# Lane work ordered behind each k-step's weight split, and lanes cut into more steps, in a hybrid encoder layer

## The chip, the cores and the metric

The kernel runs on one core of one Trainium2 chip. The metric is device time in microseconds (us) of that core; the time before is the median of three runs. The engines are named as the profile does: PE (TensorE, matrix multiplications and transposes; PEld its weight loads), DVE (VectorE), ACT (ScalarE), POOL (GpSimd) and SP (SyncE, which here only issues DMAs). Each engine runs its own list of instructions in the order in which the list stands; engines wait for each other and for DMAs by semaphores.

## The reference

One layer of an encoder over two groups of tokens, a sample of 1024 and a prompt of 256, with shared weights, and 256 memory tokens for each. The width is 2048. Cut to what matters:

```python
hn = rms_norm(x, norm_g)
xbc, z_ssd, dt_raw, q, k, v, z_att, mq, z_mem = split_cols(hn @ w_in, IN_SIZES)
xbc = silu(centred_dwconv(xbc, conv_w, conv_b))           # 5 taps along the tokens
y = ssd_scan(forward) + ssd_scan(backward) + d_skip * xs   # 16 heads, chunks of 128 tokens
o_ssd = rms_norm(y * silu(z_ssd), ssd_norm_g)              # in two groups
q, k = rms_norm(q), rms_norm(k)
o_att = window_attention(q, k, v, sink) * silu(z_att)      # |t-s| <= 128, ALiBi, 8 heads on 2
mk, mv = split_cols(rms_norm(mem) @ w_mem_kv)
mq, mk = rms_norm(mq), rms_norm(mk)
o_mem = softmax(mq @ mk.T / sqrt(128)) @ mv * silu(z_mem)  # 4 heads
return x + concat([o_ssd, o_att, o_mem]) @ w_out
```

## The kernel before, in words

The ten tiles of 128 tokens (eight of the sample, two of the prompt) are worked on in two groups of five. The large products (input projection, memory projection, output projection) are a stream of *blocks* on PE. A block takes 16 k-steps of 128 input features. Both operands are split into a high and a low part of type float32r, and each product is three matmuls: high by high, high by low, low by high. The activations of a group lie split in SBUF in four quarters (`xH`, `xL`). The weights come in k-step by k-step: SP loads `wraw` (four buffers), `wsplit` makes `wh` of it on ACT (a copy to float32r, L219, or L222 with a gain) and `wl` on DVE (the rest, L220 or L223); both have three buffers, so the split of a k-step waits until PE is done with the k-step three before it. `block_tok` (tokens on the output's partitions, up to five accumulators, matmuls L269 to L271) and `block_feat` (features on the partitions, two k-steps at a time, matmuls L304 to L306) put the matmuls out. The last two k-steps of a block are done accumulator by accumulator, and each accumulator is evicted by a function of the block's own (`ev_gate`, `ev_gateT`, `ev_raw`, `ev_dtkv`, `ev_conv`, `ev_out`, `ev_mk`, `ev_mv`), mostly to DRAM, through tiles with the tags `evt` and `evu`, two buffers each. PSUM has five buffers for accumulators (`acc`) and three for all else (`mix`).

Blocks follow each other in this order: `mk` and `mv` for the memory, then for the first group q, kv, za (2 blocks), x (6 blocks), mq, zm (2), z0, z1; for the second group kv, x (6), z0, z1, q, za (2), mq, zm (2); then four blocks of the output projection for each group.

Everything between those products is *lane work*, written as Python generators and put into two queues (`lanes`): `mem_stats` and `x_stats` (sums of squares of the rows), `vectors` and `distances` (constants), `mk_prep` and `k_prep` (norm, split and transposition of keys), `dt_prep`, `attn` (window attention of a tile of tokens), `mem_attn`, `ssd_up` (the forward scan, the diagonal part and the states of a chunk) and `ssd_down` (the backward scan and the gate). A `yield` ends a lane's *step*. `run` draws the matmuls of a block, and after each k-step `pump` lets the lanes go on, in turns, by as many steps as the rate of the block allows (`RATES`, steps for each k-step; halved in `block_feat`, which yields twice for each pair). `need` runs a lane's steps at once where its result must be there. So a program order is recorded: the split of a k-step, its matmuls, lane steps, the next split.

The order on each engine is not the recorded order. A scheduler places the instructions of each engine by priority and by its own estimate of when operands are ready. `tc.high_priority(offset=100)` moves the priority of the splits forward by 100 instructions. Nothing ties lane instructions to a split: a lane instruction whose operands are ready early in that estimate may stand on its engine long before the splits that were recorded ahead of it. Its load, DMA-issued by SP, stands on SP in the same manner.

In the lanes that the change touches, these lines matter: `mk_prep` loads a tile (L424), squares it on ACT (L428), sums it on DVE (L429), takes the inverse root on POOL (`rsqrt`, L133 and L134) and scales on DVE (L432, L433), all in one step, then leaves four steps before the transposition on PE. `k_prep` (ACT L466, DVE L467, L471, L472), `attn` (ACT L571, DVE L573, L577) and `mem_attn` (ACT L672, DVE L674, L678, PE L684) begin in the same way. `ssd_up` loads `bc` and `xc` three steps before PE uses them (L775), and its inner function `weights` loads two rows of decays, `rf` and `rb`, to all partitions, leaves one step, then adds a bias to each of 2 x 4 quarters on ACT (L848), merges them on DVE (L849) and takes the Exp on ACT (L850); `diag` multiplies with the result (L858). `vectors` loads eight constants and has `aneg` go through an Exp on ACT four steps later (L1024). `fill_transposed` (L193, L196) and `fill_direct` (L210 to L214), which fill the quarters of the next activations, are not lane steps; `run` calls them between k-steps.

Of the kernel before, what the change touches and what calls it, by code (L numbers as in the profile page):

```python
# [10 lines left out]
F32 = mybir.dt.float32  # L11
# [5 lines left out]
ALU = mybir.AluOpType  # L17
# [10 lines left out]
SCR = 1024  # L28
CH, WB, RB, WA, WBB = 3, 3, 4, 5, 4
RBB = 3  # L30
RATES = ({'kv': 1.7, 'q': 1.5, 'za': 1.5, 'x': 1.5, 'mq': 2.52, 'zm': 1.8, 'z0': 2.17, 'z1': 1.26},
         {'kv': 0.84, 'x': 1.35, 'z0': 3.81, 'z1': 2.6, 'q': 2.65, 'za': 0.93, 'mq': 2.9, 'zm': 2.54,
          'o': 2.6})
NEG = -1e30

C_X, C_Z, C_DT, C_Q, C_K, C_V, C_ZA, C_MQ, C_ZM = 0, 1536, 2560, 2592, 3104, 3232, 3360, 3872, 4384
# [4 lines left out]
def hymba_encoder_kernel(  # L41
# [106 lines left out]
    def queue(lane, fn, ts):  # L148
        for t in ts:
            lanes[lane].append(((fn.__name__, t), fn(t)))  # L150

    def step(lane):
        name, gen = lane[0]
        try:
            next(gen)
        except StopIteration:
            lane.popleft()
            done.add(name)
# [57 lines left out]
    def wsplit(raw, h, l, g=None):  # L216

        if g is None:
            A.activation(h, raw, AF.Copy)  # L219
            V.tensor_sub(l, raw, h.bitcast(F32))  # L220
        else:
            A.activation(h, raw, AF.Copy, scale=g)  # L222
            V.scalar_tensor_tensor(out=l, in0=raw, scalar=g, in1=h.bitcast(F32), op0=ALU.mult, op1=ALU.subtract)  # L223

    def w_laid(src, n, gain=None):

# [109 lines left out]

    def ev_raw(dst, base):
        def f(i, ps):
            z = ev.tile([P, 512], F32, tag="evu", name="qs")
            A.activation(z, ps, AF.Copy)  # L340
            S.dma_start(dst[base + i], z)
        return f

    def ev_dtkv(base):
        def f(i, ps):
            t = base + i
            rt = rx[:, t:t + 1]
            r = ev.tile([P, P], F32, tag="evu", name="kraw")
            A.activation(r, ps[:, 32:160], AF.Copy, scale=rt)
            S.dma_start(k_d[t], r)  # L350
            V.scalar_tensor_tensor(out=dt_all[:, t, :], in0=ps[:, :32], scalar=rt, in1=dtb, op0=ALU.mult, op1=ALU.add)
            V.tensor_scalar(out=v_all[:, i + (2 if base else 0), :], in0=ps[:, 160:288], scalar1=rt, scalar2=None,
                            op0=ALU.mult)
        return f
# [52 lines left out]
        return mp.tile([P, 512], F32, tag="wa", name=name, bufs=WA)  # L407

    def ev_mk(i, ps):
        kr = ev.tile([P, 512], F32, tag="evu", name="mkr")  # L410
        A.activation(kr, ps, AF.Copy)
        S.dma_start(mq_d[i], kr)

# [8 lines left out]
    def mk_prep(i):  # L422
        kr = w2("mkr")
        S.dma_start(kr, mq_d[i])  # L424
        ss = sm.tile([P, 4], F32, tag="s4", name="ss", bufs=4)
        sq = w2("sq")
        rm = rx[:, 10 + i:11 + i]
        A.activation(sq, kr, AF.Square, scale=rm)  # L428
        V.reduce_sum(out=ss, in_=hv(sq, 4), axis=AX.X)  # L429
        r = sm.tile([P, 4], F32, tag="s4", name="r", bufs=4)  # L430
        rsqrt(r, ss, 1.0 / P, 4)
        V.scalar_tensor_tensor(out=hv(kr, 4), in0=hv(kr, 4), scalar=rm, in1=hb(r, 4, P), op0=ALU.mult, op1=ALU.mult)  # L432
        V.tensor_mul(hv(kr, 4), hv(kr, 4), gm.unsqueeze(1).broadcast_to([P, 4, P]))  # L433
        for _ in range(4):
            yield
        ps = psum("pmk")
        for h in range(4):
            T.transpose(ps[:, h * P:(h + 1) * P], kr[:, h * P:(h + 1) * P], ident)
        c = slice((i % 2) * P, (i % 2) * P + P)
        if i < 2:  # L440
            A.activation(mkH[:, :, c], hv(ps, 4), AF.Copy)
            V.tensor_sub(mkL[:, :, c], hv(ps, 4), mkH[:, :, c].bitcast(F32))
        else:
            o = w2("mko")
            A.activation(o, ps, AF.Copy)
            S.dma_start(mk_d[:, :, c], hv(o, 4))
        yield
# [13 lines left out]
    def k_prep(t):  # L461
        r = w2("kr")[:, :P]
        S.dma_start(r, k_d[t])
        ss = sm.tile([P, 2], F32, tag="s2", name="kss", bufs=4)
        sq = w2("ksq")[:, :P]
        A.activation(sq, r, AF.Square)  # L466
        V.reduce_sum(out=ss, in_=hv(sq, 2), axis=AX.X)  # L467
        rr = sm.tile([P, 2], F32, tag="s2", name="krr", bufs=4)
        rsqrt(rr, ss, 1.0 / 64, 2)
        r3 = hv(r, 2)  # L470
        V.tensor_mul(r3, r3, hb(rr, 2, 64))  # L471
        V.tensor_mul(r3, r3, gq.unsqueeze(1).broadcast_to([P, 2, 64]))  # L472

        kh = mp.tile([P, 4, 2, 64], F32R, tag="wa", name="kh", bufs=WA)
        for d in range(2):
            A.activation(kh[:, 0:2, d, :], r3, AF.Copy)
        for d in range(2):
            V.tensor_sub(kh[:, 2:4, d, :], r3, kh[:, 0:2, 0, :].bitcast(F32))
        yield
        yield  # L480
        ps = psum("pk")
        kf = kh.rearrange("p a b d -> p (a b d)")
        for a in range(4):
            T.transpose(ps[:, a * P:(a + 1) * P].bitcast(F32R), kf[:, a * P:(a + 1) * P], identr)
        sl = t if t < 5 else t - 3
        c = slice(sl * P, (sl + 1) * P)
        V.tensor_copy(kT[:, :, c], hv(ps[:, :256], 2))
        A.activation(kL[:, :, c], hv(ps[:, 256:], 2), AF.Copy)
        yield
# [69 lines left out]
    def attn(t):  # L559
# [7 lines left out]
        tc_ = slice(ti * P, (ti + 1) * P)  # L567
        q = w2("q")
        S.dma_start(q, q_d[t])
        sq = w2("sq")  # L570
        A.activation(sq, q, AF.Square, scale=rx[:, t:t + 1])  # L571
        ss = sm.tile([P, 8], F32, tag="s8", name="qss", bufs=4)
        V.reduce_sum(out=ss, in_=hv(sq), axis=AX.X)  # L573
        r = sm.tile([P, 8], F32, tag="s8", name="qr", bufs=4)
        rsqrt(r, ss, 1.0 / 64, 8)
        q3 = hv(q)
        V.scalar_tensor_tensor(out=q3, in0=q3, scalar=rx[:, t:t + 1], in1=hb(r, 8, 64), op0=ALU.mult, op1=ALU.mult)  # L577
        yield
        yield
        yield  # L580
        qT = []
        for b in range(2):
# [83 lines left out]
    def mem_attn(t):  # L666
        grp, ti = divmod(t, 5)
        tc_ = slice(ti * P, (ti + 1) * P)
        q = w2("mq")
        S.dma_start(q, mq_d[t])  # L670
        sq = w2("sq")
        A.activation(sq, q, AF.Square, scale=rx[:, t:t + 1])  # L672
        ss = sm.tile([P, 4], F32, tag="s4", name="mss", bufs=4)
        V.reduce_sum(out=ss, in_=hv(sq, 4), axis=AX.X)  # L674
        r = sm.tile([P, 4], F32, tag="s4", name="mr", bufs=4)
        rsqrt(r, ss, 1.0 / P, 4)
        q3 = hv(q, 4)
        V.scalar_tensor_tensor(out=q3, in0=q3, scalar=rx[:, t:t + 1], in1=hb(r, 4, P), op0=ALU.mult, op1=ALU.mult)  # L678
        yield
        yield  # L680
        yield
        ps = psum("pmq")
        for h in range(4):
# [74 lines left out]
    def ssd_up(t):  # L758
# [6 lines left out]
        for g in range(2):  # L765
            x = wb("xc", shape=(P, 4, P))
            S.dma_start(x, xbc_d[4 * g:4 * g + 4, :, tok].rearrange("f p c -> p f c"))
            xc.append(x)
        yield
        yield  # L770
        yield

        ps = psum("pcb")
        for g in range(2):
# [26 lines left out]
        for g in range(2):  # L801
# [22 lines left out]
            if not first:  # L824
# [4 lines left out]
                S.dma_start(sb_d[t][:, c], st)  # L829
                yield  # L830
        mts = {}

        def weights(q):
            g = q // 2

            rf = mp.tile([P, 512], F32, tag="rf", name="rf", bufs=2)
            mt = mp.tile([P, 512], F32, tag="rb", name="rb", bufs=RBB)
            r0 = 32 * (t % 5) + 4 * q
            for d, r in enumerate((rf, mt)):
                S.dma_start(r, ac_d[t // 5][r0 + 16 * d:r0 + 16 * d + 4, :]  # L840
                            .rearrange("h c -> (h c)").partition_broadcast(P))
            yield

            for d, r in enumerate((rf, mt)):
                for j in range(4):
                    c = slice(j * P, (j + 1) * P)
                    h = 16 * d + 4 * q + j
                    A.activation(r[:, c], r[:, c], AF.Identity, bias=wj_all[:, t, h:h + 1])  # L848
            V.copy_predicated(hv(mt, 4), upper.bitcast(U32).unsqueeze(1).broadcast_to([P, 4, P]), hv(rf, 4))  # L849
            A.activation(mt, mt, AF.Exp)  # L850
            V.tensor_mul(hv(mt, 4), hv(mt, 4), cb[:, g, :].unsqueeze(1).broadcast_to([P, 4, P]))
            mts[q] = mt

        def diag(g):
# [9 lines left out]
            V.tensor_add(ya[g], ya[g], py)  # L864
            S.dma_start(yp_d[t][:, g * 512:(g + 1) * 512], ya[g])

        for q in range(3):
            yield from weights(q)
            yield
        diag(0)  # L870
        yield
        yield from weights(3)
        yield
        yield
        diag(1)
# [136 lines left out]
    def vectors(_):  # L1012
        gk, gmk = w2("gk")[:, :64], w2("gmk")[:, :P]
        for t, a in ((gq, q_norm_g[0]), (gk, k_norm_g[0]), (gm, mq_norm_g[0]), (gmk, mk_norm_g[0]),
                     (dskip, d_skip[0]), (sinkb, sink[0]), (dtb, dt_bias.rearrange("o a h -> (o a h)")),
                     (aneg, a_log.rearrange("o a h -> (o a h)"))):
            S.dma_start(t, a.partition_broadcast(P))
        yield
        yield
        yield  # L1020
        yield
        V.scalar_tensor_tensor(out=gq, in0=gq, scalar=64 ** -0.5, in1=gk, op0=ALU.mult, op1=ALU.mult)
        V.scalar_tensor_tensor(out=gm, in0=gm, scalar=P ** -0.5, in1=gmk, op0=ALU.mult, op1=ALU.mult)
        A.activation(aneg, aneg, AF.Exp)  # L1024
        V.tensor_scalar(out=aneg, in0=aneg, scalar1=-1.0, scalar2=None, op0=ALU.mult)
        yield
# [153 lines left out]
```

## Time and profile before

| what | us |
|---|---|
| median of three runs | 1917.64 (1916.83 to 1919.4) |
| profiled execution, its own time | 1925.01 |
| profiled execution, span of the core | 1923.3 |
| PE busy | 1875.9 (98% of the span) |
| DVE busy | 1049.4 (55%) |
| ACT busy | 760.9 (40%) |
| POOL busy | 81.6 (4%) |
| DMA, mean share of 16 engines on the main queue | 48.9% |

The span runs from the first to the last instruction. Busy time is a union, so overlapping matmuls count once. The views used below are the page of the profile, the view of waits (who waited for whom, total, times and longest), the order of time of one engine in a stretch, and the table of stretches with the busy time and count of each engine, the clock granted to PE (1.00 is full), the share of the DMA engines and GB/s.

### The profile page before, as it was taken

The page shows a single profiled execution, that of the slowest core. Times are in us where ns is not written, and L with a number is a line of the kernel's source. Part 1 is how long each engine was busy: PE and PEld are TensorE (multiplying, and loading weights), DVE is VectorE, ACT ScalarE, POOL GpSimd, SP SyncE. Part 2 cuts the span into 40 slices and gives each one's busy share as a digit, 9 for nine tenths or more (in the row PEclk, how much of TensorE's full clock was granted, in tenths as well). Part 3 has the DMA queues.
Part 4 walks back from the last instruction along what each step waited for, and adds up shares of the span by engine and source line. Part 5 has one row for each costly group of instructions (what it writes and reads, how often), then busy time and mean ns, then how long its engine had stood idle before and what let it go on. Part 6 is the DMA issues. An engine that isn't in the chain of part 4 may idle for free.

```text
span 1923.3 us, 28675 instructions
## 1 busy us (share of the span) xinstructions
PE 1875.9 (98%) x10568; PEld 1634.2 (85%) x10568; DVE 1049.4 (55%) x2133; ACT 760.9 (40%) x1721; POOL 81.6 (4%) x147
## 2 busy tenths in 40 slices
PE   8999989999999999999999999999999999999999
PEld 6779989998898879999978778978978787778887
DVE  4443646677564555667776554576675454542222
ACT  6462463333452545423436444334453333421121
POOL 1010010000000000000100000000000000000000
PEclk9999999999999999999999999999999999999999
DMA  8683563233343545433444567655555345454432
GB/s 272 198 257 104 157 182 121 85 114 109 116 124 113 154 140 172 138 96 101 140 131 142 158 177 247 209 187 162 170 158 186 123 149 159 136 176 132 133 120 69
DMA packets 191340, 289.40 MB, mean 150 GB/s; under 512 B 18977, under 2 KB 68193, under 8 KB 191201
## 3 DMA queue, kind: packets, MB, share of 16 engines
q1 hardware_dynamic: 191056, 287.53, 48.9%
q8 instruction: 83, 1.36, 0.3%
q14 instruction: 57, 0.46, 0.1%
q10 hardware_dynamic: 144, 0.06, 0.0%
HBM read 230.59 MB, written 56.92 MB: 149 GB/s over the span
## 4 chain that ended last, share of the span: by engine, by line
PE 77%; DMA 11%; ACT 4%; DVE 4%; issue 2%; POOL 1%; SPq 1%; ACTq 0%; DVEq 0%; POOLq 0%
PE acc L269 14%; PE acc L270 14%; PE acc L271 14%; PE acc L304 8%; PE acc L305 8%; PE acc L306 8%; DMA xst<-in_x_sample_dram 2%; DMA rf<-ac 2%; PE po L648 2%; PE py L858 1%; PE ppt L637 1%; DMA rb<-ac 1%; DVE wl L220 1%; PE pst L826 1%; PE pst L817 1%
## 5 line engine op out<-in xcount | busy, mean ns | idle before, releaser
L269 PE MATMUL acc<-wh,xH 128*128 128x512 f32 (+1 forms) x1568 | 619.0, 395 | 9.0 <-ACT wh L219 5.6
L270 PE MATMUL acc<-wl,xH 128*128 128x512 f32 (+1 forms) x1568 | 601.6, 384 | 2.9 <-DVE wl L220 2.7
L271 PE MATMUL acc<-wh,xL 128*128 128x512 f32 (+1 forms) x1568 | 600.3, 383 | 0.0
L220 DVE TENSOR_TENSOR wl<-wraw,wh 128x512 fp32r<-128x512 f32 (+1 forms) x416 | 278.3, 670 | 384.4 <-ACT wh L219 376.1
L219 ACT ACTIVATE wh<-wraw 128x512 fp32r<-128x512 f32 (+1 forms) x416 | 254.1, 612 | 528.7 <-PE acc L271 268.0
L304 PE MATMUL acc<-xH,wh 128*128 128x320 f32 x1280 | 406.1, 317 | 9.0 <-DVE zs L331 4.7
L306 PE MATMUL acc<-xH,wl 128*128 128x320 f32 x1280 | 396.6, 310 | 1.6 <-DVE wl L220 1.4
L305 PE MATMUL acc<-xL,wh 128*128 128x320 f32 x1280 | 396.6, 310 | 0.0
L269 PEld LDWEIGHTS acc<-wh,xH 128*128 128x128 f32 x1568 | 296.4, 189 | 69.2 <-issue 8.4
L270 PEld LDWEIGHTS acc<-wl,xH 128*128 128x128 f32 x1568 | 296.7, 189 | 62.9 <-issue 6.6
L271 PEld LDWEIGHTS acc<-wh,xL 128*128 128x128 f32 x1568 | 296.2, 189 | 56.5 <-issue 0.6
L304 PEld LDWEIGHTS acc<-xH,wh 128*128 128x128 f32 x1280 | 241.3, 189 | 15.0 <-DVE zs L331 5.2
L305 PEld LDWEIGHTS acc<-xL,wh 128*128 128x128 f32 x1280 | 241.3, 189 | 3.3 <-issue 3.2
L306 PEld LDWEIGHTS acc<-xH,wl 128*128 128x128 f32 x1280 | 241.1, 188 | 2.3 <-DVE wl L220 2.3
L223 DVE SCALAR_TENSOR_TENSOR wl<-wraw,vec,wh 128x512 fp32r<-128x512 f32 x64 | 48.0, 750 | 128.0 <-ACT wh L222 128.0
L222 ACT ACTIVATE wh<-wraw,vec 128x512 fp32r<-128x512 f32 x64 | 46.3, 723 | 145.4 <-PE acc L271 132.3
L379 DVE SCALAR_TENSOR_TENSOR c<-u,vec,c 128x638 f32<-128x638 f32 (+1 forms) x96 | 84.5, 880 | 1.0
L848 ACT ACTIVATE rb<-rb,wj_all 128x128 f32<-128x128 f32 x160 | 53.0, 391 | 49.1 <-DMA rb<-ac 46.5
L848 ACT ACTIVATE rf<-rf,wj_all 128x128 f32<-128x128 f32 x160 | 53.6, 390 | 33.5 <-DMA rf<-ac 33.5
L622 ACT ACTIVATE lg<-lg,nm 128x384 f32<-128x384 f32 (+1 forms) x80 | 45.1, 564 | 46.2 <-DVE nm L616 46.1
L849 DVE COPY_PREDICATED rb<-upper,rf 128x512 f32<-128x512 uint32 x40 | 30.3, 757 | 53.0 <-ACT rb L848 52.8
L214 DVE SCALAR_TENSOR_TENSOR xL<-chd,vec,xH 128x640 fp32r<-128x640 f32 (+1 forms) x48 | 39.6, 837 | 23.5 <-ACT xH L213 23.5
(238 smaller groups left out, 1725.5 us busy)
## 6 DMA issues: line engine op xcount, KB each, us to landing
wraw<-in_w_in_laid_dram SPq DMA_DIRECT2D x288, 256.0 KB, 2.8
wraw<-in_w_out_laid_dram SPq DMA_DIRECT2D x128, 256.0 KB, 2.7
chd<-in_x_turned_dram SPq DMA_DIRECT2D x32, 320.0 KB, 4.1
rf<-ac SPq DMA_DIRECT2D x40, 256.0 KB, 3.8
rb<-ac SPq DMA_DIRECT2D x40, 256.0 KB, 4.2
out_dram<-yt SPq DMA_DIRECT2D x40, 256.0 KB, 3.6
wraw<-in_w_mem_laid_dram SPq DMA_DIRECT2D x32, 256.0 KB, 4.3
xst<-in_x_sample_dram SPq DMA_DIRECT2D x32, 256.0 KB, 4.9
```

Source lines behind the costliest of these rows:

```text
L219: A.activation(h, raw, AF.Copy)
L220: V.tensor_sub(l, raw, h.bitcast(F32))
L222: A.activation(h, raw, AF.Copy, scale=g)
L223: V.scalar_tensor_tensor(out=l, in0=raw, scalar=g, in1=h.bitcast(F32), op0=ALU.mult, op1=ALU.subtract)
L269: T.matmul(ps[t][:, :n], sh, h[:, :n], start=(k_ == 0), stop=False)
L270: T.matmul(ps[t][:, :n], sh, l[:, :n], start=False, stop=False)
L271: T.matmul(ps[t][:, :n], sl, h[:, :n], start=False, stop=(k_ == KT - 1))
L304: T.matmul(o, sh, cur["H", q][:, m, c], start=(k == 0), stop=False)
L305: T.matmul(o, sh, cur["L", q][:, m, c], start=False, stop=False)
L306: T.matmul(o, sl, cur["H", q][:, m, c], start=False, stop=(k == KT - 1))
L379: V.scalar_tensor_tensor(out=c[:, :n], in0=u[:, k:k + n], scalar=cw[k], in1=c[:, :n], op0=ALU.mult, op1=ALU.add)
L848: A.activation(r[:, c], r[:, c], AF.Identity, bias=wj_all[:, t, h:h + 1])
```

## The change

Four things are changed. `wsplit` keeps its two instructions in `marks`, and each lane step is recorded inside `tc.issue_after` for both: every ACT instruction of the step gets an ordering edge behind that k-step's `wh`, and every DVE instruction one behind its `wl`. No semaphore comes with the edge; it only sets the order on the engine. Second, lanes get further `yield`s between a load, POOL's inverse root and their users, `ssd_up` splits `weights` into `rows` (the loads, one call ahead) and `weights` (the rest), waits six steps instead of three for `bc` in tiles 0 and 4, and `vectors` waits six. Third, `ev_raw`, `ev_dtkv` and `ev_mk` alternate between the tags `evt` and `evu`. Fourth, the rates are set anew, most of them higher.

```diff
-RATES = ({'kv': 1.7, 'q': 1.5, 'za': 1.5, 'x': 1.5, 'mq': 2.52, 'zm': 1.8, 'z0': 2.17, 'z1': 1.26},
-         {'kv': 0.84, 'x': 1.35, 'z0': 3.81, 'z1': 2.6, 'q': 2.65, 'za': 0.93, 'mq': 2.9, 'zm': 2.54,
-          'o': 2.6})
+RATES = ({'kv': 1.8, 'q': 1.7, 'za': 1.7, 'x': 1.7, 'mq': 2.7, 'zm': 1.9, 'z0': 2.4, 'z1': 1.6},
+         {'kv': 1.0, 'x': 1.4, 'z0': 3.7, 'z1': 2.8, 'q': 2.8, 'za': 1.3, 'mq': 2.8, 'zm': 2.4,
+          'o': 2.65})
...
+    marks = []
+
     def step(lane):
         name, gen = lane[0]
         try:
-            next(gen)
+
+            with ExitStack() as st:
+                for ins in marks:
+                    st.enter_context(tc.issue_after(ins))
+                next(gen)
         except StopIteration:
...
     def wsplit(raw, h, l, g=None):
 
         if g is None:
-            A.activation(h, raw, AF.Copy)
-            V.tensor_sub(l, raw, h.bitcast(F32))
+            a = A.activation(h, raw, AF.Copy)
+            b = V.tensor_sub(l, raw, h.bitcast(F32))
...
+        marks[:] = a.ins, b.ins
...
     def ev_raw(dst, base):
         def f(i, ps):
-            z = ev.tile([P, 512], F32, tag="evu", name="qs")
+            z = ev.tile([P, 512], F32, tag="evt" if i % 2 else "evu", name="qs")
...
     def mk_prep(i):
         kr = w2("mkr")
         S.dma_start(kr, mq_d[i])
+        yield
...
         rsqrt(r, ss, 1.0 / P, 4)
+        yield
+        yield
         V.scalar_tensor_tensor(out=hv(kr, 4), in0=hv(kr, 4), scalar=rm, in1=hb(r, 4, P), op0=ALU.mult, op1=ALU.mult)
         V.tensor_mul(hv(kr, 4), hv(kr, 4), gm.unsqueeze(1).broadcast_to([P, 4, P]))
-        for _ in range(4):
-            yield
+        yield
+        yield
...
     def k_prep(t):
         S.dma_start(r, k_d[t])
+        yield
...
         rsqrt(rr, ss, 1.0 / 64, 2)
+        yield
...
     def attn(t):   # and mem_attn(t) in the same way
         S.dma_start(q, q_d[t])
+        yield
...
         rsqrt(r, ss, 1.0 / 64, 8)
+        yield
         q3 = hv(q)
         V.scalar_tensor_tensor(out=q3, in0=q3, scalar=rx[:, t:t + 1], in1=hb(r, 8, 64), op0=ALU.mult, op1=ALU.mult)
-        yield
-        yield
         yield
...
     def ssd_up(t):
-        yield
-        yield
-        yield
+        for _ in range(6 if t in (0, 4) else 3):
+            yield
...
-        for q in range(3):
-            yield from weights(q)
-            yield
-        diag(0)
-        yield
-        yield from weights(3)
-        yield
-        yield
-        diag(1)
-        yield
+        rows(0)
+        yield
+        for q in range(3):
+            if q < 2:
+                rows(q + 1)
+                yield
+            weights(q)
+            yield
+        diag(0)
+        rows(3)
+        yield
+        yield
+        weights(3)
+        yield
+        yield
+        diag(1)
+        yield
...
     def vectors(_):
-        yield
-        yield
-        yield
-        yield
+        for _ in range(6):
+            yield
         V.scalar_tensor_tensor(out=gq, in0=gq, scalar=64 ** -0.5, in1=gk, op0=ALU.mult, op1=ALU.mult)
         V.scalar_tensor_tensor(out=gm, in0=gm, scalar=P ** -0.5, in1=gmk, op0=ALU.mult, op1=ALU.mult)
+        yield
         A.activation(aneg, aneg, AF.Exp)
```

More of the change, by code (lines that the diff above doesn't have):

```diff
@@ L218, in wsplit @@
         if g is None:
-            A.activation(h, raw, AF.Copy)
-            V.tensor_sub(l, raw, h.bitcast(F32))
-        else:
-            A.activation(h, raw, AF.Copy, scale=g)
-            V.scalar_tensor_tensor(out=l, in0=raw, scalar=g, in1=h.bitcast(F32), op0=ALU.mult, op1=ALU.subtract)
+            a = A.activation(h, raw, AF.Copy)
+            b = V.tensor_sub(l, raw, h.bitcast(F32))
+        else:
+            a = A.activation(h, raw, AF.Copy, scale=g)
+            b = V.scalar_tensor_tensor(out=l, in0=raw, scalar=g, in1=h.bitcast(F32), op0=ALU.mult,
+                                       op1=ALU.subtract)
+        marks[:] = a.ins, b.ins
     def w_laid(src, n, gain=None):
@@ L347, in f @@
             rt = rx[:, t:t + 1]
-            r = ev.tile([P, P], F32, tag="evu", name="kraw")
+            r = ev.tile([P, P], F32, tag="evt" if i % 2 else "evu", name="kraw")
             A.activation(r, ps[:, 32:160], AF.Copy, scale=rt)
@@ L409, in ev_mk @@
     def ev_mk(i, ps):
-        kr = ev.tile([P, 512], F32, tag="evu", name="mkr")
+        kr = ev.tile([P, 512], F32, tag="evt" if i % 2 else "evu", name="mkr")
         A.activation(kr, ps, AF.Copy)
@@ L831, in ssd_up, with rows @@
         mts = {}
-        def weights(q):
-            g = q // 2
+        rows_ = {}
+        def rows(q):
             rf = mp.tile([P, 512], F32, tag="rf", name="rf", bufs=2)
@@ L841, in weights @@
                             .rearrange("h c -> (h c)").partition_broadcast(P))
-            yield
+            rows_[q] = rf, mt
+        def weights(q):
+            g = q // 2
+            rf, mt = rows_.pop(q)
             for d, r in enumerate((rf, mt)):
```

## The prediction

> **What bounds the kernel now.** The page comes first: its busy line, the chain of work that ended last, and the rows of TensorE's costliest groups.
>
> ```profile
> span 1923.3 us, 28675 instructions
> PE 1875.9 (98%) x10568; PEld 1634.2 (85%) x10568; DVE 1049.4 (55%) x2133; ACT 760.9 (40%) x1721; POOL 81.6 (4%) x147
> PE 77%; DMA 11%; ACT 4%; DVE 4%; issue 2%; POOL 1%; SPq 1%; ACTq 0%; DVEq 0%; POOLq 0%
> ```
>
> TensorE (PE) is busy in all but 1923.3 − 1875.9 = 47.4 us, so only that idle time, and time spent at a reduced clock, can be gained while its instructions stay the same. DVE and ACT have half their time free. Yet 11% of the last chain is DMA: some transfer is waited for by an engine that PE then waits for. Who PE waits for stands in the view of waits, PE alone, whole span (total us, times, longest):
>
> ```profile
> PE acc L269 <- ACT wh L219: 5.6, 1, 5.6
> PE acc L304 <- DVE zs L331: 4.7, 2, 4.4
> PE pr L196 <- DVE ch L193: 3.9, 3, 1.4
> PE pmq L684 <- issue: 3.9, 2, 2.6
> PE acc L269 <- ACT mkr L411: 3.4, 1, 3.4
> PE pcb L775 <- DMA bc<-xbc_d: 3.2, 2, 2.4
> PE acc L270 <- DVE wl L220: 2.7, 4, 1.0
> PE ppt L637 <- DVE lg L627: 2.4, 2, 1.6
> PE acc L304 <- DVE u L363: 2.0, 2, 1.8
> PE po L648 <- ACT pT L638: 1.5, 1, 1.5
> PE acc L306 <- DVE wl L220: 1.4, 2, 1.0
> PE pst L826 <- DVE xb L810: 1.4, 1, 1.4
> PE py L858 <- DVE rb L851: 1.2, 2, 0.9
> PE acc L304 <- DVE u L371: 0.9, 1, 0.9
> PE acc L304 <- ACT kraw L349: 0.6, 1, 0.6
> ```
>
> The first row is the start, before any weight is split; nothing in the change touches it. The others are some thirty short stops. Each looks like a late ACT or DVE instruction, so the next question is what that engine did just before. Views of the order of time, ACT at 50 to 60 us and DVE at 135 to 148 us, then ACT at 1020 to 1024 us (start, duration, instruction, idle time before it and who ended it):
>
> ```profile
> 50.49 1.06 ACT L411 ACTIVATE mkr<-acc 128x512 f32<-128x512 f32 x2
> 56.56 0.23 ACT L1024 ACTIVATE aneg<-aneg 128x32 f32<-128x32 f32 x1 [5.01 <-DMA aneg<-in_a_log_dram]
> 57.98 0.60 ACT L411 ACTIVATE mkr<-acc 128x512 f32<-128x512 f32 x1 [1.19 <-DMA mq<-mkr]
> ```
> ```profile
> 136.55 0.75 DVE L432 SCALAR_TENSOR_TENSOR mkr<-mkr,rx,r 128x512 f32<-128x512 f32 x1 [1.44 <-POOL r L134]
> 137.22 0.68 DVE L220 TENSOR_TENSOR wl<-wraw,wh 128x512 fp32r<-128x512 f32 x1
> ```
> ```profile
> 1022.62 1.28 ACT L848 ACTIVATE rb<-rb,wj_all 128x128 f32<-128x128 f32 x4 [4.76 <-DMA rb<-ac]
> 1023.80 0.60 ACT L622 ACTIVATE lg<-lg,nm 128x384 f32<-128x384 f32 x1
> ```
>
> One pattern in all three: a lane instruction waits at the head of its engine for a DMA (5.01 us, 4.76 us) or for POOL (1.44 us), while work that PE needs (mkr's eviction, wl, attention's lg) stands behind it. Over the whole span, ACT's waits:
>
> ```profile
> ACT wh L219 <- PE acc L271: 268.0, 118, 5.5
> ACT wh L219 <- PE acc L305: 164.9, 78, 5.5
> ACT rb L848 <- DMA rb<-ac: 46.5, 23, 4.8
> ACT rf L848 <- DMA rf<-ac: 33.5, 23, 4.3
> ACT xst L928 <- DMA xst<-in_x_sample_dram: 15.6, 13, 3.8
> ```
>
> The rf and rb loads alone hold ACT for 80 us. Most ACT idle time is harmless: the split waits for PE to free a wh buffer (433 us).
>
> The stops also cost clock. Stretches of time (busy time and count of each engine, then PEclk, DMA share, GB/s):
>
> ```profile
> 58.00:61.50 3.50, 2.87 (x7) 2.30 (x8) 1.81 (x3) 2.73 (x5) 0.00 (x0) 0.50 0.42 104
> 61.50:64.90 3.40, 3.40 (x10) 2.63 (x9) 0.17 (x1) 0.00 (x0) 0.00 (x0) 0.52 0.84 279
> 64.90:68.30 3.40, 3.40 (x17) 2.79 (x16) 0.69 (x1) 0.99 (x2) 0.00 (x0) 1.00 0.12 30
> 259.30:266.20 6.90, 5.51 (x22) 5.47 (x23) 4.15 (x11) 4.88 (x14) 0.61 (x1) 0.51 0.81 256
> 1402.80:1406.20 3.40, 3.40 (x14) 2.81 (x14) 2.12 (x5) 0.60 (x1) 0.00 (x0) 0.50 0.91 320
> 1631.50:1634.90 3.40, 3.40 (x10) 2.63 (x9) 0.69 (x1) 0.55 (x1) 0.00 (x0) 0.50 0.79 270
> ```
>
> After the 3.4 us stop before 58.6 us PE runs at half clock: 10 matmuls in 3.4 us against 17 at full clock. Work at clock 0.5 loses half its time, so the four places lose about (2.87 + 3.40)/2 = 3.1, 5.51/2 = 2.7, 1.7 and 1.7 us: 9.2 us. All that could be gained is then 47.4 − 5.6 (start) − the tail, some 35 to 40 us of stops, plus 9.
>
> [...]
>
> **The change part by part.** Instruction counts are equal on every engine (ACT, DVE, SP, POOL, PE), and so are the DMAs; only order moves. Read from the order of both built programs: on ACT 408 of 1042 non-split instructions stood ahead of the split of the k-step in which they were recorded, 227 of them by ten k-steps or more; now none. A first user of an rf (rb) load stood only one split behind it in 28 (29) cases of 40; now in 4 (7). For xst it is 20 before and 5 after. Loads are not tied to the splits, so they stay early and only the users move back. Lane steps grow from 756 to 789; the rates grow with them, and the two steps that had to be forced ahead of the last refill become none.
>
> Gains, by row, and how much of each I take:
> - vectors (aneg's Exp six more steps behind its load) and ev_mk's second buffer pair (mkr need not wait for a store): 3.4 us of L269 <- mkr, and 3.1 us of clock. ACT then holds statistics squares there (mst), which may wait on their loads. Take 5 of 6.5.
> - mk_prep in more steps: the three wl stops of 135 to 148 us, nearly all of the 2.7 us. Take 2.5.
> - k_prep in more steps, rf/rb no longer hoisted into block za: zs 4.7 us and clock 2.7 us. Take 5 of 7.4.
> - attn's load, square and scaling in separate steps, xst farther from its load: u L363 2.0 us and part of wl L306. Take 1.5.
> - ssd_up(0) and (4) wait six steps, not three, for bc: 3.2 us. The gap per stop was at most 2.4 us; three more steps are more than one k-step of 15 matmuls (3.4 us at the 17-matmul row). Take 3.
> - rows one to two steps ahead of weights: the stops behind rf/rb loads are ppt 2.4, xb 1.4, rb 1.2, one wl of 1.0: 6.0 us. Take 4.5.
> - q's load (po 1.5), u L371 0.9, kraw 0.6: 3.0 us. Take 2.
> - pmq 3.9 us and 1.7 us of clock: mem_attn has as many steps between load and transpose as before, but the last scaling now stands one step before the transpose instead of three. It can shrink to nothing or grow by another stop of 1.4 us each. Take 0.
> - pr 3.9 us: fill_transposed is no lane step. Take 0.
>
> Sum of gains: 5 + 2.5 + 5 + 1.5 + 3 + 4.5 + 2 = 23.5 us.
>
> Costs. Lane work that used to run in idle ACT time many k-steps early now stands in its own step. No row of before shows these new meetings, so they are bounded. The near case is DVE at x-block boundaries: attention now starts where the eviction of block x3 puts its convolution on DVE, and by the new order wl of x4's fourth split stands behind both. The nearest rows:
>
> ```profile
> L379 DVE SCALAR_TENSOR_TENSOR c<-u,vec,c 128x638 f32<-128x638 f32 (+1 forms) x96 | 84.5, 880 | 1.0
> 300.00:460.00 160.00, 160.00 (x1120) 154.87 (x1119) 111.89 (x241) 53.76 (x118) 6.09 (x7) 1.00 0.34 104
> L848 ACT ACTIVATE rb<-rb,wj_all 128x128 f32<-128x128 f32 x160 | 53.0, 391 | 49.1 <-DMA rb<-ac 46.5
> ```
>
> Before, the same kind of boundary with attention beside it cost PE nothing from 300 to 460 us (160.00 busy of 160), which is the lower end. The upper end is that every second one of the later ones stops PE as long as the worst acc stop did, about 4 us: five times 4 is 20 us. I take 8 us, 2 to 3 us for x4 and the rest in small stops and a clock drop, because the row of no stop is the same work on the same engine. Four more returns from lane work to matmuls (277 against 273) are under 1 us.
>
> Net: 23.5 − 8 = 15.5. The profiled execution took 1925.01 us (span 1923.3 and 1.7 around it), 7.4 us or 0.4% above the median of the three runs, 1917.64. So about 1909.5 profiled, and 1917.64 − 15.5, rounded to **1902 us** as a median.
>
> **The rivals.**
> - *The stops only change place.* Each stop removed lets PE arrive earlier at the next lane result, and that is late by as much. For it: stops are spread over all stages; pr and pmq remain. Against it: 300 to 460 us shows a stage with lanes and no stop at all. All gains go but the early ones to 148 us (7.5), and the 8 us of new stops remain: about 1917 to 1919.
> - *Slower: weights bursts held behind the split.* A call of weights is eight activations of 0.39 us and an Exp, about 3.7 us of ACT. Before, most of the 40 ran early; now each stands in the heavy stages, behind a split that itself waits for PE (the 433 us) and ahead of the other lane's exponentials and evictions. Place: blocks mq to z1, Z0 to Q, MQ to o1. If a burst delays PE by its own 3.7 us, six of 40 eat the 23.5 us of gains; at ten, 37 − 23.5 gives about 1931, and more with clock drops. Against it: ACT is 40% busy, and PE reaches a split's product two k-steps, some 7 us, after ACT may begin it. [...]
> - *More is gained.* The full rows (35.5 us by the list above, pmq included) and few new stops: about 1884.
>
> **How the numbers follow.** Forecast 0.62 (own range 1892 to 1912), more gained 0.10, stops change place 0.13, slower 0.15. No change that a measurement could tell is within 0.2%, 1913.8 to 1921.5. So faster 0.72, same 0.12, slower 0.16. The range 1886 to 1926 leaves out the lower half of the third rival's gains and most of the slower case, under 0.2.
>
> **What would show it.** Right: ACT's waits for rf and rb fall from 80 us to under 20, aneg's 5.01 us and mkr's 3.4 us are gone, pcb no longer waits for bc, the half-clock stretches at 58 and 259 us are gone, and PE's idle time is near 30 us. Wrong: ACT or DVE results of a lane (ppt, po, pms, psc) or wl wait rows of several us each in blocks x4, Z0 to Q and o0, with exponentials behind rf/rb activations; or PE idle time still near 47 us under other names; or new half-clock stretches.

## The result and the profile after

The changed kernel takes 1890.99 us (median of four runs, 1889.62 to 1892.4); the kernel before, run beside it, 1918.52 us (1916.83 to 1923.84). The ratio is 0.9839, interval 0.9819 to 0.986: 27.5 us faster, where 15.5 were forecast. The profiled execution took 1890.37 us.

The page of the changed kernel (span, busy times, chain that ended last):

```profile
span 1888.3 us, 28679 instructions
PE 1867.4 (99%) x10568; PEld 1631.8 (86%) x10568; DVE 1056.7 (56%) x2133; ACT 760.1 (40%) x1721; POOL 80.7 (4%) x147
PE 94%; DVE 2%; DMA 2%; ACT 1%; issue 1%; POOL 0%; SPq 0%; DVEq 0%; ACTq 0%
```

PE's idle time fell from 47.4 us to 1888.3 − 1867.4 = 20.9 us, and DMA from 11% of the last chain to 2%. The spans differ by 35.0 us: 26.5 of idle time and 8.5 of PE's busy time, for the same 10568 matmuls. This pair flatters the change, because the profiled execution of before lay 0.4% above its median; the ratio is what counts. The waits of PE after (total us, times, longest):

```profile
PE acc L277 <- ACT wh L225: 5.3, 1, 5.3
PE pmq L697 <- issue: 3.2, 1, 3.2
PE pst L838 <- DVE ya L825: 2.2, 1, 2.2
PE ppt L650 <- DVE lg L640: 1.7, 1, 1.7
PE py L874 <- DVE rb L867: 1.4, 2, 0.8
PE pr L202 <- DVE ch L199: 1.3, 1, 1.3
PE pmt L735 <- DVE mpr L727: 0.5, 1, 0.5
PE acc L277 <- DVE zs L329: 0.5, 1, 0.5
PE psc L620 <- DVE lg L622: 0.3, 1, 0.3
PE pcb L787 <- DMA bc<-xbc_d: 0.2, 1, 0.2
```

Nothing is left of the stops on mkr, wl, u, po and xb. New are `pst <- ya` and two of 0.5 us (pmt, and zs of another line). The one ppt has the name of two stops of before, at 1026 and 1423 us, and another place: 443.9 us. That is not the boundary at x4 that the prediction named. The six x blocks are evicted at 266, 294, 323, 352, 389 and 422 us, so it lies in block mq, 20 us behind the last of them, and PE does not stop once between its start and there. DVE at the last of these evictions, and just before the stop:

```profile
422.27 0.49 DVE L371 TENSOR_TENSOR u<-acc,rbc 128x320 f32<-128x320 f32 x1 [1.64 <-PE acc L314]
```
```profile
441.79 0.75 DVE L592 SCALAR_TENSOR_TENSOR q<-q,rx,qr 128x512 f32<-128x512 f32 x1 [1.81 <-POOL qr L134]
442.73 0.69 DVE L226 TENSOR_TENSOR wl<-wraw,wh 128x512 fp32r<-128x512 f32 x1
443.33 0.74 DVE L640 TENSOR_SCALAR lg<-lg,den 128x384 f32<-128x384 f32 x2
```

attn's scaling waits 1.81 us for POOL, and the lg that the ppt needs stands behind it. From ACT's waits after:

```profile
ACT wh L225 <- PE acc L279: 285.8, 124, 6.4
ACT wh L225 <- PE acc L313: 168.1, 86, 4.6
ACT rb L864 <- DMA rb<-ac: 31.6, 9, 4.5
ACT xst L951 <- DMA xst<-in_x_sample_dram: 5.2, 5, 1.9
ACT rf L864 <- DMA rf<-ac: 2.7, 3, 1.4
```

rf and rb together wait 34.3 us instead of 80; the split's slack, its wait for PE to free a buffer, grew in these two rows from 433 to 454 us.

The new stop of `pst` in order of time (start, duration, instruction, idle time before it), DVE from 1365 us and PE:

```profile
1365.28 0.75 DVE L592 SCALAR_TENSOR_TENSOR q<-q,rx,qr 128x512 f32<-128x512 f32 x1 [2.04 <-POOL qr L134]
1365.95 0.48 DVE L199 TENSOR_SCALAR ch<-ch,rs_all 128x512 f32<-128x512 f32 x1
1366.34 0.68 DVE L226 TENSOR_TENSOR wl<-wraw,wh 128x512 fp32r<-128x512 f32 x1
1366.94 0.68 DVE L825 TENSOR_TENSOR ya<-pyf,eacs_all 128x512 f32<-128x512 f32 x1
```
```profile
1367.68 1.61 PE L838 MATMUL pst<-xb,btok 128*128 128x512 f32 x2 [2.18 <-DVE ya L825]
```

It is the old pattern, and the one of 443.9 us: attn's scaling waited 2.04 us for POOL with a split and `ya` behind it. The clock, at the places of the first two falls of before, then in the window ahead of each remaining fall and the window behind it (length, then busy us of PE, PEld, DVE, ACT, POOL, then PEclk):

```profile
58.00:66.00 8.00, 8.00 (x37) 6.63 (x36) 3.97 (x7) 4.07 (x6) 0.00 (x0) 1.00 0.38 99
259.00:267.00 8.00, 8.00 (x57) 8.00 (x56) 2.86 (x7) 2.36 (x6) 0.95 (x3) 1.00 0.35 101
1364.78:1368.19 3.41, 1.23 (x7) 0.76 (x6) 2.91 (x6) 1.39 (x3) 0.46 (x1) 1.00 0.57 166
1368.19:1371.60 3.41, 3.41 (x12) 2.85 (x11) 2.36 (x6) 0.60 (x1) 0.00 (x0) 0.50 0.44 144
1603.71:1607.12 3.41, 1.37 (x8) 1.12 (x9) 0.83 (x3) 0.60 (x1) 1.07 (x2) 1.00 0.68 234
1607.12:1610.53 3.41, 3.41 (x15) 3.31 (x15) 2.22 (x5) 0.63 (x1) 0.00 (x0) 0.50 0.15 47
```

The half-clock stretches at 58 and 259 us are gone. Two of 3.4 us are left, behind `pst` and behind `pmq`, against 20.5 us in sum before.

### The profile page after: what moved, and what is told of

Same layout as the page of the kernel before. It is cut to its first block, busy times and chain, and to the rows that moved or that the text cites. A ratio compares the mean times of both kernels' runs of the same rounds, so it can differ in the third digit from the quotient of the medians.

```text
span 1888.3 us, 28679 instructions
## 1 busy us (share of the span) xinstructions
PE 1867.4 (99%) x10568; PEld 1631.8 (86%) x10568; DVE 1056.7 (56%) x2133; ACT 760.1 (40%) x1721; POOL 80.7 (4%) x147
## 4 chain that ended last, share of the span: by engine, by line
PE 94%; DVE 2%; DMA 2%; ACT 1%; issue 1%; POOL 0%; SPq 0%; DVEq 0%; ACTq 0%
PE acc L277 17%; PE acc L278 17%; PE acc L279 17%; PE acc L312 10%; PE acc L314 10%; PE acc L313 10%; PE po L661 2%; PE py L874 2%; PE ppt L650 1%; PE pmo L748 1%; PE pst L838 1%; PE pst L829 1%; PE pyb L929 1%; PE pyf L824 1%; PE psc L620 1%
## 5 line engine op out<-in xcount | busy, mean ns | idle before, releaser
L622 DVE SCALAR_TENSOR_TENSOR lg<-ndist,psc 128x384 f32<-128x384 bf16 (+1 forms) x80 | 38.1, 495 | 24.0 <-PE psc L621 24.0
```

## The experiments

They were run in three groups, each beside runs of the kernel before on the same chip (median 1910.31, 1912.07 and 1921.74 us). Ratios are compared within a group first.

| group | kernel | us | ratio, interval |
|---|---|---|---|
| 1 | edges alone | 1889.53 | 0.9898, 0.9875 to 0.992 |
| 1 | all but the edges | 1911.22 | 1.0, 0.9988 to 1.0012 |
| 1 | all, edge behind `wh` only | 1888.34 | 0.9888, 0.9869 to 0.9906 |
| 1 | all, old rates | 1894.45 | 0.9921, 0.9904 to 0.9939 |
| 2 | the changed kernel | 1885.6 | 0.9863, 0.9845 to 0.988 |
| 2 | edge behind `wl` alone | 1899.22 | 0.9933, 0.9914 to 0.9951 |
| 2 | edges for ssd_up's steps alone | 1907.12 | 0.9972, 0.996 to 0.9984 |
| 2 | edges for all other lanes | 1893.3 | 0.9899, 0.9878 to 0.992 |
| 3 | edges alone, loads late | 1903.77 | 0.9913, 0.9889 to 0.9937 |
| 3 | changed kernel, loads late | 1893.66 | 0.9868, 0.9838 to 0.9898 |
| 3 | edges and new rates | 1899.17 | 0.989, 0.9865 to 0.9915 |
| 3 | changed kernel with more steps | 1881.54 | 0.9799, 0.9776 to 0.9822 |

And PE's stops by what was late (us, summed over the rows of the view of waits; "eviction" means the accumulator's matmuls waiting for it; a dash is no row; what never passes 1 us is left out). Each column is one execution. That of `c1_after`, the changed kernel again, has the same kinds of stops as "after" with each sum within 1.0 us, but no half-clock window (its mean granted clock is 1.0, that of "after" 0.998):

| | before | after | edges alone | all but edges | edges, loads late | more steps |
|---|---|---|---|---|---|---|
| mkr eviction | 3.4 | – | – | 2.4 | 0.6 | – |
| wl | 4.1 | – | – | 2.2 | – | – |
| zs eviction | 4.7 | 0.5 | 1.3 | 6.3 | 1.6 | 1.5 |
| u | 2.9 | – | – | 0.5 | – | – |
| bc (pcb) | 3.2 | 0.2 | 1.4 | – | 1.6 | 1.1 |
| ppt, po, xb, rb | 6.8 | 3.1 | 1.9 | 5.9 | 9.8 | 1.8 |
| prx, xL | 2.8 | – | 0.6 | – | – | – |
| ya | – | 2.2 | – | 0.5 | – | – |
| pr | 3.9 | 1.3 | 3.0 | 2.3 | 4.6 | 1.1 |
| pmq | 3.9 | 3.2 | 3.5 | 2.7 | 2.8 | – |
| half-clock windows of 3.4 us | 6 | 2 | 1 | 5 | 3 | 0 |

**The edges and the rest.** The prediction credited most of the gain to the further steps, rows and buffers, edit by edit. The first pair separates them.

```diff
# edges alone: the kernel before, and
+    marks = []
...
+            with ExitStack() as st:
+                for ins in marks:
+                    st.enter_context(tc.issue_after(ins))
+                next(gen)
...
+        marks[:] = a.ins, b.ins
# all but the edges: the changed kernel, and
-        marks[:] = a.ins, b.ins
+        marks[:] = []
```

> The kernel before with the ordering edges alone: steps, rates, buffers as before. Theory O (the edges do it, because ACT and DVE instructions of a lane no longer stand right behind their own loads at the head of the engine): by the order of the built program, first users of rf and rb one split behind their load fall from 28 and 29 of 40 to 5 and 8, nearly as in the changed kernel, so three quarters of the gain, about 1897 us; ACT's waits for rf and rb under 45 us in place of 80. The three bc and mkr stops (3.2 and 3.4 us) may stay. Theory S (the further steps do it, the edges add little): within 5 us of before, 1914 to 1922, with PE's idle time near 47 us.

> The changed kernel without the ordering edges; further steps, rates and buffers stay. Theory O: the scheduler hoists lane work again (412 ACT instructions ahead of the split of their step, 30 and 21 rf and rb users one split behind their load), so 1905 to 1915 us and ACT's waits for rf and rb at 60 us or more; the bc and mkr stops stay away. Theory S: within 5 us of the changed kernel, 1886 to 1896.

Measured: 0.9898 with the edges alone, a larger gain than the 1897 us that theory O gave them, and 1.0 with everything but the edges, where mkr's stop was expected to stay away and 2.4 us of it are there. ACT's order at 50 to 58 us shows why, without the edges first, then with them alone:

```profile
50.61 1.06 ACT L419 ACTIVATE mkr<-acc 128x512 f32<-128x512 f32 x2
56.48 0.23 ACT L1046 ACTIVATE aneg<-aneg 128x32 f32<-128x32 f32 x1 [4.81 <-DMA aneg<-in_a_log_dram]
```
```profile
49.21 0.60 ACT L419 ACTIVATE mkr<-acc 128x512 f32<-128x512 f32 x1 [0.76 <-PE acc L279]
52.79 0.60 ACT L419 ACTIVATE mkr<-acc 128x512 f32<-128x512 f32 x1 [2.98 <-DMA mq<-mkr]
```

With seven steps between load and Exp in place of four, but no edge, the Exp still stands among the evictions of `mk` and waits 4.81 us (5.01 before). With the edges and the old steps no wait of `aneg` is left, and the `mkr` eviction, which now waits 2.98 us for its one buffer pair, stops PE not at all. ACT's waits without the edges:

```profile
ACT rb L864 <- DMA rb<-ac: 47.1, 26, 4.2
ACT rf L864 <- DMA rf<-ac: 33.4, 27, 3.0
```

80.5 us, as before: without the edges the rows issued one call ahead gave nothing. A `yield` is a distance in the recorded order only. The scheduler that sets the engines' order moves the user up again as soon as it believes the operands ready. In the programs as built, 412 of ACT's lane instructions stood ahead of the split of their own k-step without the edges (408 before, none with them).

**On which engine, and for which lanes.**

```diff
# edge behind wh only: the changed kernel, and
-        marks[:] = a.ins, b.ins
+        marks[:] = [a.ins]
# edge behind wl alone: edges alone, and
-        marks[:] = a.ins, b.ins
+        marks[:] = [b.ins]
# ssd_up alone (== ), all other lanes (!= ): edges alone, and
-                for ins in marks:
+                for ins in marks if name[0] == "ssd_up" else ():
```

> The changed kernel with the edge behind wh alone: lane instructions of DVE are free to stand ahead of wl (117 do, in place of 58). If the waits at the head of ACT are the cause, the time is that of the changed kernel, 1888 to 1895. If DVE's waits for POOL and ACT ahead of wl matter as much, wl stops come back (2 to 5 us of PE waiting for wl in total) and the time is 1895 to 1903.

> The kernel before with the edge behind wl alone, on DVE; ACT is free to hoist (345 lane instructions ahead of the split of their step, rf and rb users one split behind their load in 33 and 29 cases of 40). If waits at the head of ACT are the cause, no gain: 0.998 to 1.002 of before. If the order on DVE is enough, 0.988 to 0.993.

The changed kernel with ACT's edge only reaches 0.9888 and has no stop on wl: lane work on DVE often follows an ACT instruction of the same lane, and so, it seems, moves with it (117 of DVE's lane instructions stand ahead of their split, 58 with both edges). The order on DVE alone gives 0.9933: neither nothing nor all. Its trace keeps `aneg`'s wait:

```profile
56.40 0.23 ACT L1032 ACTIVATE aneg<-aneg 128x32 f32<-128x32 f32 x1 [4.87 <-DMA aneg<-in_a_log_dram]
```

and a 2.9 us stop on mkr with it, yet the stop on u is gone and wl is down to 0.2 us. The heads that block stand on both engines. ACT's edge alone on the old steps wasn't run.

> The changed kernel itself, beside the next three on one chip. On the chip of the first four runs the edges alone reached 0.9898 of before. If the further steps, rows, buffers and rates add something to the edges, this comes out at 0.984 to 0.987; if they add nothing, at 0.988 to 0.992.

> The kernel before with edges for the steps of ssd_up alone (rf, rb). Theory H (waits at the head of ACT, priced by the stops behind each load): the rf and rb stops are about 6 us of PE's 42, and zs in block za with its half clock another 5 to 7, so a third of the gain: 0.994 to 0.997 of before. If the rf and rb loads are the whole cause (80 us of ACT's waits, the largest DMA wait), 0.988 to 0.991.

> The complement: edges for every lane but ssd_up. Theory H: the early stops (mkr, wl, u, x and za evictions) with their half clock go, two thirds of the gain: 0.992 to 0.995 of before. If rf and rb are the whole cause, 0.998 to 1.001.

The changed kernel gave 0.9863 on this chip. With edges for ssd_up alone 0.9972, for all other lanes 0.9899. Theory H, which priced the stops, gave the first too much (0.994 to 0.997) and the second too little (0.992 to 0.995); that rf and rb are the whole cause is refuted by both. The second leaves ACT's largest DMA waits as they were:

```profile
ACT rb L856 <- DMA rb<-ac: 43.7, 23, 4.3
ACT rf L856 <- DMA rf<-ac: 30.9, 23, 6.8
```

74.6 us of waiting at ACT's head, and the ratio is that of the edges alone on another chip (0.9898). So the row of ACT's waits that looked largest was mostly harmless; the edges on ssd_up gave 0.3% while the other lanes had none. Most of the gain lies in the other lanes, whose waits are short (aneg, the norms of mk_prep and k_prep, attn's query); they were not parted further.

**Distance to the load, or place behind the split?** The edges move the user and leave the load early, so the user lies further behind its load; but a lane instruction that waits *behind* the split also has the whole of ACT's slack ahead of the next one (the splits' wait for PE, 454 us in sum after). To part the two, the loads of mk_prep, k_prep, attn, mem_attn, rf and rb were issued from ACT, where the edge holds them too. (That also takes them out of SP's list, where the median issue of each took 0.32 to 0.43 us before, and gives ACT the work of issuing them; this part was not separated.)

```diff
-        S.dma_start(q, q_d[t])
+        A.dma_start(q, q_d[t])
# likewise kr of mk_prep, r of k_prep, q of mem_attn, rf and rb
```

> The kernel before with the edges of the change alone, but the loads of the lanes mk_prep, k_prep, attn, mem_attn and the rows rf and rb are issued from ACT, so that the edges hold the loads behind the split too, and a load is no longer issued ahead of the split that its user waits for. Theory D (the edges gain because the load keeps its early place on SP and only its user moves behind the split, so that the transfer of some 2 us lies beside the split): most of the gain is lost, the time is 0.996 to 1.010 of before, ACT again waits over 60 us in sum for rows, q, mq and kr, and waits of wh behind these appear in the waits of PE. Theory S (it is the place behind the split alone that counts, since what waits behind the split no longer holds that split up): the time stays at 0.988 to 0.993 of before, as with the edges alone, although ACT waits longer for the loads.

> The changed kernel with the same loads issued from ACT behind the split: here one further step lies between load and user. Theory D: the further step gives back the distance that the late issue takes, so the time is 0.984 to 0.990 of before, and this run stands at least 0.5% under the one with late loads and the old steps. Theory S: within 0.3% of the changed kernel and also within 0.3% of the run with late loads and the old steps, if that run kept its gain.

The transfers that theory D put at some 2 us took 3.1 to 4.2 us in the trace of before, median from issue to landing (q and mkr 3.1, kr 3.2, rf 3.8, mq 4.0, rb 4.2). ACT's waits with the edges alone and late loads:

```profile
ACT rb L856 <- DMA rb<-ac: 32.6, 17, 6.1
ACT sq L680 <- DMA mq<-mq: 17.5, 9, 3.4
ACT rf L856 <- DMA rf<-ac: 15.0, 9, 3.5
ACT sq L579 <- DMA q<-q: 12.6, 7, 2.3
```

These four wait 77.7 us, and the first three rows alone 65.1 us, against 23.6 + 1.2 + 4.7 = 29.5 us for the same three with early loads. Still 18.0 us of the gain remain (1921.74 to 1903.77), of 22.6 with early loads and the new rates (1899.17; the edges alone were not run on this chip). So about four fifths of what the edges give is the place behind the split: the stops on wl and u stay away with late loads, and those on zs and mkr stay small (table). The distance is the smaller share, and its place shows too: ppt, po, xb and rb cost 9.8 us here. The rest of the change then works: the changed kernel with the same late loads is 10.1 us faster (1893.66; the ranges, 1891.9 to 1896.4 and 1901.1 to 1904.0, lie apart), about the 0.5% that theory D asked of the further step, though rates, rows and buffers differ as well. Neither theory alone was right.

**Rates and steps.**

> The changed kernel with the rates of before: 33 more steps at the old pace, so lanes end later and steps are forced ahead of the last refill. Theory O: rates are not the cause; 1890 to 1900 us, the loss being a stop where steps are forced at the fourth output block. Rival R (the higher rates make the gain): 1908 us or more.

> The kernel before with the edges and the new rates alone, with the old steps, buffers and rows. If what the changed kernel has over the edges alone (some 0.3%) comes from the rates, this run stands at 0.985 to 0.987 of before; if it comes from the further steps, rows and buffers, it stays at 0.988 to 0.991.

The new rates come to nothing with the old steps (0.989, against 0.9898 for the edges alone on another chip), and the new steps with the old rates are 4.9 us slower than the edges alone on the same chip (1894.45 against 1889.53, ranges apart): `pr` stops 4.7 us and `ppt` 2.7 us. With 33 steps more to draw at the old rates, lane work comes later than PE wants it; that reading is argued, not tested. What both together add to the edges was not measured side by side. Across chips it is 0.3 to 0.6%, by intervals that overlap for one of the two (0.9875 to 0.992 against 0.9845 to 0.988); the nearest pair on one chip, all with ACT's edge only against the edges alone, is 1888.34 against 1889.53 us, no difference.

**A version that is faster.** Three stops of after looked like matters of distance: `ppt` and `pst` behind POOL's qr, and `pmq`. The load of `pmq` was issued at 1596.61 us, ACT's first user waited for it, and the last scaling on DVE stood right before the transposition at 1605.75:

```profile
1601.68 0.72 ACT L686 ACTIVATE sq<-mq,rx 128x512 f32<-128x512 f32 x1 [6.12 <-DMA mq<-mq]
1604.90 0.75 DVE L693 SCALAR_TENSOR_TENSOR mq<-mq,rx,mr 128x512 f32<-128x512 f32 x1 [1.18 <-POOL mr L134]
```

```diff
# the changed kernel, and (cut to what matters; attn also gets the second yield behind its rsqrt)
     def mem_attn(t):
         S.dma_start(q, mq_d[t])
-        yield
+        for _ in range(3 if t >= 5 else 1):
+            yield
...
         rsqrt(r, ss, 1.0 / P, 4)
+        yield
         yield
# RATES: mq 2.8, zm 2.0, z0 2.45, z1 1.7; x 1.45, z0 3.75, mq 2.85, zm 2.5, o 2.85
```

> The changed kernel with more distance where its trace still shows stops: the load of mem_attn stands three steps ahead of its user for t of 5 and over, one more step stands behind the rsqrt of attn and of mem_attn, and the rates of the lanes are raised a little to make room. If the remaining stops of PE (pmq 3.21 with the half clock that follows, pst 2.18 with the half clock that follows, py 1.4, pr 1.3) are each a matter of distance, 4 to 8 us go, and the time is 0.982 to 0.984 of before; if the further steps only move lane work to splits where it stops PE elsewhere, it stays at 0.985 to 0.989.

Measured 1881.54 us, 0.9799 (0.9776 to 0.9822), a little better than expected, and than the changed kernel on either chip where that ran (0.9839, 0.9863); on this chip it did not run. Beside the edges with the new rates, on the same chip, it is 17.6 us faster (1899.17). The page, then PE's waits:

```profile
span 1878.3 us, 28639 instructions
PE 1861.3 (99%) x10568; PEld 1628.1 (87%) x10568; DVE 1055.5 (56%) x2133; ACT 761.1 (41%) x1721; POOL 82.8 (4%) x147
```
```profile
PE acc L277 <- ACT wh L225: 5.2, 1, 5.2
PE py L877 <- DVE rb L870: 1.5, 3, 0.9
PE acc L277 <- DVE zs L329: 1.5, 3, 0.6
PE pcb L790 <- DMA bc<-xbc_d: 1.1, 1, 1.1
PE pr L202 <- DVE ch L199: 1.1, 1, 1.1
```

The stops on pmq, ppt and ya are gone, nothing but the start stops PE longer than 1.1 us, and the mean granted clock is 1.0 (0.994 before). For `pmq` it was not the distance to the load that did it: ACT still waits 3.98 us for that load, until 1600.02 us, but the transposition now stands at 1607.33, four us behind the scaling. Further steps do pay once an edge makes them hold; the rates, raised again, were not parted from them.

## Why the prediction was right or wrong

Right were the sign, the wide range (1886 to 1926), and the pattern: a lane instruction that waits at the head of ACT or DVE with PE's work behind it. The time, 1891, lies one microsecond outside the forecast's own range (1892 to 1912), towards the rival "more is gained" (1884). The steps in turn:

- *"Vectors and ev_mk's second buffer pair", 5 of 6.5 us: size right, cause wrong.* Stop and half-clock stretch are gone, but the edges alone do it, with four steps and one buffer pair. The change puts Exp three steps further behind its load (seven for four), not six, and without the edges these leave 4.81 us of wait and a 2.4 us stop.
- *"mk_prep in more steps" 2.5, "k_prep in more steps" 5, "attn's steps" 1.5, "q's load" 2: the same error.* Without the edges wl keeps 2.2 us of stops, zs 6.3 and po 2.7; only u falls, to 0.5. With them alone wl, u and po have none and zs 1.3. The error is one step of the argument: a `yield` was read as a distance on the engine, though the description of the kernel said that the recorded order is not the engine's.
- *"Loads stay early and only the users move back": half right.* It is true, and it is not the main reason. With loads as late as their users the edges keep four fifths of their gain.
- *"Rows one to two steps ahead of weights", 4.5 of 6.0 us: size near, cause wrong.* The stops of ppt and xb that were counted there are gone, those of rb are not (1.4). But the waits for rf and rb fell to 34.3 us, not under 20, and with 74.6 us of them left in place the ratio is still that of the edges alone.
- *bc, 3 of 3.2 us: the stop went as forecast; its cause stays open.* It is 0.2 after and absent without the edges, but 1.4 with the edges and three steps, and 1.8 with six steps and late loads.
- *pr, taken as 0: under-rated.* It fell from 3.9 to 1.3 us. fill_transposed is no lane step, but its DVE work shares the queue with lane work. Which part of the change does it was not found: 3.0 with the edges alone, 2.3 without them, 4.7 with the old rates.
- *pmq, taken as 0: right* (3.9 to 3.2 us, still with a half-clock window).
- *New stops, 8 us: size near, by luck; place and mechanism wrong.* The 2 to 3 us at x4, wl behind x3's convolution, did not come: PE does not stop there. What came is ppt 1.7 in block mq and ya 2.2, both behind attn's scaling, which waits for POOL with one step between; pmt and zs 0.5 each make 4.9, and the window behind ya costs 1.7: 6.6 us.
- *The clock: the loss of 9.2 us was nearly right, and the part regained under-rated.* Six windows before and two after make 4 × 1.7 = 6.8 us (the window behind ya, counted above, is one of the two). The window of 1402.8 us was in the loss and in no row of the gains.
- *Rows that no gain was counted for.* The stops of prx and of py behind xL, 1.4 us each, are gone, and with the second its window, 1.7: 4.5 us.

The under-sizing of 12 us therefore has several sources. The largest are the discounts, some 6 us: each row was discounted because its own edit might not remove it, while one edit removes nearly all rows at once. pr and pmq give 3.3 us more, and the rows that were not counted 4.5. That is more than 12, and against it stands an error the other way: the rows were read in an execution 7.4 us above the median and taken off the median. (The full list of gains, pmq and its clock included, adds up to 36.4 us, not 35.5.) Of the rivals, "stops only change place" is refuted by PE's idle time of 20.9 us. The burst of weights behind a split, priced at 3.7 us for each one that delays PE, shows at most as `py <- rb`: 1.4 us in two stops. That the slack named against it covers the rest is argued, not tested.

## What to carry to other kernels

Where a scheduler sets the order of the engines, a distance written into the program holds only if an ordering edge pins the user; the edge costs no instruction (ACT 1721 and DVE 2133 before and after). Here the edges alone gave 1.0% of the 1.4 to 1.6% in all, and everything else without them nothing. Of the waits at an engine's head, price those that have work for the bounding engine behind them and no slack, not the largest sum: 75 us of waits for rf and rb cost nothing that the ratios show, and one of 5 us for a vector of 32 cost a stop of 3.4 us and two windows, 6.8 us, of half clock. Pin first, and then add steps where the trace still shows a head that waits; steps gave nothing without the pin, and with it, rates along with them, 0.5% and 0.9% side by side on one chip (late loads; more steps).

## What was not expected of the hardware

In the trace of before the half-clock stretches begin at 57.94, 259.33, 1402.79 and 1631.48 us, the first two 6.83 us long and the others 3.41, so the later ones begin 59, 394 and 461 times 3.413 us behind the first; in that of after they begin at 1368.19 and 1607.12 us, 70 times 3.413 us apart. Cut into windows of 3.413 us from these starts, from 10 us to PE's last matmul, the two traces together have five windows at full clock with 2.04 to 3.07 us of PE's idle time, and a half-clock window follows each; of 13 with 1.0 to 1.8 us, it follows one, that of 1.37 us ahead of 1402.79 us. One of 1.79 us, from 293.46 us, was not followed, so in these two traces a window's idle time does not decide it alone, and neither does the length of a stop. A stop of 2.41 us before 983.6 us, in the trace of before, lies across two windows:

```profile
979.54:982.95 3.41, 1.66 (x8) 1.04 (x6) 0.77 (x2) 1.46 (x6) 0.00 (x0) 1.00 0.33 100
982.95:986.37 3.42, 2.77 (x20) 2.50 (x20) 1.79 (x4) 0.54 (x2) 0.00 (x0) 1.00 0.17 63
986.37:989.78 3.41, 3.41 (x18) 2.53 (x17) 3.41 (x9) 0.86 (x2) 0.00 (x0) 1.00 0.33 75
```

1.75 us fell into the first window and 0.65 into the second, and the clock stayed at 1.00; the stop of 2.18 us in the changed kernel lay within one window (1364.78 to 1368.19 above), and the next had a clock of 0.50. The same program in `c1_after` stopped 2.2 us for pmq, at a mean granted clock of 1.0. So a stop of 2.2 to 2.4 us cost itself alone or another 1.7 us, half of the 3.41 at clock 0.50. What makes the clock fall, and whether that is part of why runs of one kernel differ by some microseconds, was not shown.
